# Norms by scaled tokens and plain transposes, attention heads placed ahead of the block-inverse merges

## The chip, the cores and the metric

The kernel runs on one core of one Trainium2 chip, as one launch. The metric is the device time of that core in microseconds (us). The kernel before was run three times: 1037.62, 1032.43 and 1036.91 us, median 1036.91. One more execution was recorded by the profiler; every row of a trace below is from that one.

## The reference, cut to what matters

All arithmetic is f32. The input is 256 tokens of width 1024. Three layers follow one another; the first two are layers 0 and 1 of a transformer (mixers of kind MLA and differential attention), the third is a hybrid of attention and a gated delta rule.

```python
def rms_norm(x, g):
    return x * rsqrt(mean(x * x, -1) + EPS) * g

for i in range(2):                                   # layers 0 and 1
    a = mixer_i(rms_norm(h, norm_g[i, 0]))           # MLA, then differential attention
    h = h + rms_norm(a, norm_g[i, 1])
    f = conv_ffn(rms_norm(h, norm_g[i, 2]))          # up 1024->5632, conv of width 3, gelu gate, down
    h = h + rms_norm(f, norm_g[i, 3])

# hybrid layer
p = rms_norm(h, pre_norm_w) @ w_in                   # q,k,v,z of two branches, beta, decay, two gates
o_a = causal_attention(rope(q_a), rope(k_a), v_a)    # 8 heads of 128
q_b, k_b, v_b = silu(causal_conv4(...))              # width 4, per channel
g = -exp(a_log) * softplus(decay + dt_bias);  beta = sigmoid(...)
# per head and chunk: strict lower triangular m[i,j] = beta_i k_i.k_j exp(G_i - G_j)
#   (I + m) is inverted, and the state passes from chunk to chunk
o_b = rms_norm(gated_delta_rule(q_b, k_b, v_b, g, beta), gdn_norm_w)
y = sigmoid(gate_a) * ((o_a * silu(z_a)) @ w_a) + sigmoid(gate_b) * ((o_b * silu(z_b)) @ w_b)
out = h + rms_norm(y @ w_out, post_norm_w)
```

## The kernel before

**Data.** The residual `h` has tokens on the partitions, in two blocks `tb` of 128 tokens. What a matmul consumes is transposed: `xT` has channels on the partitions, 8 tiles `kt` of 128 channels by 256 tokens. Nearly all products are done in three passes (`mm3`, lines 131 to 133): an f32 operand is split into a rounded high part `hi` and a remainder `lo`, and hi*hi, hi*lo and lo*hi are added. `wload` fetches weights from memory in 512 KB pieces through SyncE's queue into a ring of `RB = 5` slots; ScalarE makes the high part (L116), VectorE the low part (L117). `split` (L125) does the same for activations.

**A norm.** `boundary` stands between two stages. `postnorm` adds a stage's normed output to `h`. `prenorm` makes ready the next stage's normed input: ScalarE squares and sums (L199, in `square`), VectorE computes 1/rms in six small steps (`newton`, L208 to L221). Beside that, VectorE multiplies the left half of the tokens with the norm weight into `hg[0]` (L278) and GpSimd the right half into `hg[1]` (L279). VectorE then scales the identity by 1/rms into the diagonal `dg` (L282). `turn` multiplies each 128x128 piece of `hg` by `dg` on TensorE (L290): that scales and transposes in one product. The first norm has no weight of its own at this point; its `hg` is `h` itself, and the weight is put in behind the turn, as `gT`. There are five such norms (into MLA, FFN, differential attention, FFN, hybrid) of two token blocks each. The second block's `prenorm` stands behind the first block's splits (`ends`). In both FFN stages the first two column pairs of the up-projection run in plain f32 from `xF` (L602).

**The hybrid layer.** Eight times `h_kq` projections with their convolution; then for 2 chunks x 2 groups of 4 heads: decay matrices (L953 to L962), products k.k and k.q (L967), from them the matrices `A` and `Bm` (L971, L973), and `turn_A` (L946, L947), which transposes a group's `A` into `M` one group after it was made. `M`'s 16x16 diagonal blocks go through a scratch in memory (L985, L987), VectorE inverts them in 15 steps (L992, L993), the result goes through the scratch again, twice (L999, L1001), and is expanded to the block diagonal `V` and its transpose `VT` by a product with a mask (L1003; `V` on VectorE, `VT` on GpSimd). Then four projections `v_b`; three merge levels (L1038 to L1060) that grow the inverted blocks from 16 to 128; the delta rule's products (L1073); and eight attention heads (L1117 to L1157), each with a projection, rope (L1124 to L1127), softmax and products, and a gate projection `zproj` on every second one. After the heads come the two branches' projections and the output.

**Order.** The program is traced in the order of its text and a planner orders each engine's instructions by their place in the text and by its own model of when their inputs are ready; an instruction later in the text runs earlier when the one ahead isn't ready in that model. On the chip each engine and each DMA queue then runs its list in order. `behind(x)` forces the instructions in its block to stand after `x` on `x`'s engine.

Of the kernel before, what the change touches and what calls it, by code (L numbers as in the profile page):

```python
# [17 lines left out]
P = 128  # L18
# [19 lines left out]
def build(tc, a, out):  # L38
# [246 lines left out]
    def turn(tb, hg, dg, xT, xF=None):  # L285
# [466 lines left out]
    def hybrid(xT, fin):  # L752
        with ExitStack() as c2:
# [129 lines left out]
            last_mm = []  # L883
# [65 lines left out]
            pend = None  # L949
            for c in range(2):  # L950
                for gr in range(2):
# [46 lines left out]
            for src, sc, dst, eng in ((TBt, scr[2], V, nc.vector), (TB, scr[1], VT, nc.gpsimd)):  # L998
                nc.sync.dma_start(sc.rearrange("y b r s -> (y b) r s"), src)  # L999
                cb = lt("MB" if dst is V else "cbt", [P, 16, 16])  # L1000
                nc.sync.dma_start(cb, sc.rearrange("y b r s -> (b r) y s"))  # L1001
                for c in range(2):
                    eng.tensor_tensor(dst[:, c].rearrange("p n (b s) -> p n b s", b=8),  # L1003
                                      cb[:, 8 * c:8 * c + 8, None, :].to_broadcast([P, 8, 8, 16]),
                                      bmask.rearrange("p (b s) -> p b s", b=8)[:, None].to_broadcast([P, 8, 8, 16]),
                                      op=ALU.mult)

            def v_b(hp):
                b = proj2(wload(a["h_vb"][hp], 2048), (mmb, mmb, lambda: bank("s"), lambda: bank("s"))[hp])
                c = pair(0)  # L1010
                for t in range(2):
                    conv4(b[:, t], 16 + 2 * hp + t, c[:, t])
                th = pair(1)
                nc.scalar.activation(th, c, AF.Tanh, scale=0.5)
                nc.vector.scalar_tensor_tensor(c, th, 1.0, c, op0=ALU.add, op1=ALU.mult)
                for tb in range(2):
                    b = smb()
                    for t in range(2):
                        nc.tensor.transpose(b[:, t * P:(t + 1) * P], c[:, t, tsl[tb]], ident)
                    nc.vector.tensor_tensor(Vik[:, tb, 2 * hp:2 * hp + 2], b[:, :S].rearrange("p (t s) -> p t s", t=2),  # L1020
# [326 lines left out]
```

## Time and profile before

| | |
|---|---|
| median of 3 runs | 1036.91 us (1032.43 to 1037.62) |
| profiled execution | 1035.35 us, span 1033.4 us |
| TensorE matmul | busy 1008.6 us, 98% of the span, 7116 instructions |
| TensorE weight load | 923.6 us, 89% |
| VectorE | 739.4 us, 72% |
| ScalarE | 547.6 us, 53% |
| GpSimd | 33.3 us, 3% |
| memory traffic | 162.70 MB, 157 GB/s on average |
| granted TensorE clock | 0.995 of full on average |

Matmuls are pipelined: the busy time of one is its length from start to result, and the next begins before it ends. What a stream of them costs is read from the distance between starts. Waits and the chain of work that ended last say where another engine sets the pace.

### The profile page before, as it was taken

Reading aid. Unit: us, or ns where it says so; the run is one execution under the profiler, and the core shown is the slowest. Engines: PE = TensorE matmul, PEld = TensorE weight load, DVE = VectorE, ACT = ScalarE, POOL = GpSimd, SP = SyncE. Lnnn points to the kernel's source line nnn. Section 1 sums busy time; section 2 is a strip of 40 time slices with the busy share of each in tenths; the row PEclk is TensorE's granted clock in tenths of the full one; section 3 lists DMA queues with packets and bytes.
Section 4 is the critical chain, followed back from the end, with each engine's and each line's share of the span. In section 5 each row is a group of like instructions: output and inputs, shape, how many; then the busy total and the mean of one; then the engine's idle time right before and its main releaser. Section 6 shows DMA issues by size and latency. Waiting matters only on the chain.

```text
span 1033.4 us, 18142 instructions
## 1 busy us (share of the span) xinstructions
PE 1008.6 (98%) x7116; PEld 923.6 (89%) x7116; DVE 739.4 (72%) x1391; ACT 547.6 (53%) x955; POOL 33.3 (3%) x35
## 2 busy tenths in 40 slices
PE   9989899999999999999999999999999999999997
PEld 6878799999987887799999997899898999999996
DVE  6785688777667578778777767488799657675564
ACT  5653466555536456566555555565554455544451
POOL 0000100000011000010000001000203000000000
PEclk9999899999999999999999999999999999999999
DMA  8473477655435335367655442545244413455551
GB/s 280 148 238 110 145 226 213 188 185 165 135 96 200 136 102 183 96 235 229 209 189 187 146 143 75 172 156 174 71 146 101 132 61 115 151 184 184 185 164 42
DMA packets 55301, 162.70 MB, mean 157 GB/s; under 512 B 12784, under 2 KB 15280, under 8 KB 55216
## 3 DMA queue, kind: packets, MB, share of 16 engines
q1 hardware_dynamic: 55216, 161.55, 48.8%
q8 instruction: 56, 0.92, 0.4%
q14 instruction: 29, 0.24, 0.1%
HBM read 160.08 MB, written 1.44 MB: 156 GB/s over the span
## 4 chain that ended last, share of the span: by engine, by line
PE 85%; DVE 8%; ACT 3%; DMA 2%; issue 1%; SPq 0%; POOL 0%; DVEq 0%; ACTq 0%; POOLq 0%
PE mm L131 11%; PE mm L132 11%; PE mm L133 11%; PE acc L132 8%; PE acc L131 8%; PE acc L133 8%; PE sm L133 4%; PE sm L132 4%; PE sm L131 4%; PE mm L602 3%; PE acc L1038 2%; DVE lo L117 1%; PE acc L1073 1%; PE sm L290 1%; PE s L718 1%
## 5 line engine op out<-in xcount | busy, mean ns | idle before, releaser
L117 DVE TENSOR_TENSOR lo<-raw,hi 128x1024 fp32r<-128x1024 f32 (+1 forms) x271 | 326.8, 1209 | 137.6 <-ACT hi L116 136.4
L116 ACT CAST hi<-raw 128x1024 fp32r<-128x1024 f32 (+1 forms) x271 | 278.1, 1035 | 243.5 <-PE mm L132 126.4
L133 PE MATMUL mm<-xT,lo 128*128 128x256 f32 x928 | 265.7, 286 | 0.0
L131 PE MATMUL mm<-xT,hi 128*128 128x256 f32 x928 | 265.3, 286 | 0.0
L132 PE MATMUL mm<-xT,hi 128*128 128x256 f32 x928 | 265.0, 286 | 0.0
L132 PEld LDWEIGHTS mm<-xT,hi 128*128 128x128 f32 x928 | 177.6, 191 | 1.9 <-issue 0.7
L131 PEld LDWEIGHTS mm<-xT,hi 128*128 128x128 f32 x928 | 177.5, 191 | 1.5 <-issue 0.3
L133 PEld LDWEIGHTS mm<-xT,lo 128*128 128x128 f32 x928 | 177.6, 191 | 1.3 <-issue 0.7
L131 PE MATMUL sm<-xT,hi 128*128 128x256 f32 (+1 forms) x328 | 92.9, 283 | 0.0
L133 PE MATMUL sm<-xT,lo 128*128 128x256 f32 (+1 forms) x328 | 92.8, 283 | 0.0
L132 PE MATMUL sm<-xT,hi 128*128 128x256 f32 (+1 forms) x328 | 92.8, 283 | 0.0
L131 PE MATMUL acc<-hi,gv 128*128 128x512 f32 x176 | 69.2, 393 | 0.3 <-ACT gv L125 0.3
L132 PE MATMUL acc<-lo,gv 128*128 128x512 f32 x176 | 69.0, 392 | 0.0
L133 PE MATMUL acc<-hi,gv 128*128 128x512 f32 x176 | 68.5, 389 | 0.0
L132 PEld LDWEIGHTS sm<-xT,hi 128*128 128x128 f32 (+1 forms) x328 | 62.2, 190 | 0.9
L131 PEld LDWEIGHTS sm<-xT,hi 128*128 128x128 f32 (+1 forms) x328 | 62.2, 190 | 0.8
L133 PEld LDWEIGHTS sm<-xT,lo 128*128 128x128 f32 (+1 forms) x328 | 62.2, 190 | 0.1
L133 PEld LDWEIGHTS acc<-hi,gv 128*128 128x128 f32 x176 | 33.1, 188 | 7.5 <-DVE gv L125 0.3
L131 PEld LDWEIGHTS acc<-hi,gv 128*128 128x128 f32 x176 | 33.2, 189 | 6.6 <-ACT gv L125 1.0
L132 PEld LDWEIGHTS acc<-lo,gv 128*128 128x128 f32 x176 | 33.2, 189 | 5.3
L131 PE MATMUL mm<-og,hi 128*128 128x256 f32 x128 | 36.0, 281 | 0.0
L132 PE MATMUL mm<-og,hi 128*128 128x256 f32 x128 | 36.0, 281 | 0.0
(489 smaller groups left out, 1892.8 us busy)
## 6 DMA issues: line engine op xcount, KB each, us to landing
raw<-in_ffn_up SPq DMA_DIRECT2D x88, 512.0 KB, 4.7
raw<-in_ffn_down SPq DMA_DIRECT2D x44, 512.0 KB, 4.3
raw<-in_diff_qk SPq DMA_DIRECT2D x16, 512.0 KB, 5.0
raw<-in_h_kq SPq DMA_DIRECT2D x16, 512.0 KB, 4.6
raw<-in_h_qk SPq DMA_DIRECT2D x16, 512.0 KB, 4.3
raw<-in_h_z SPq DMA_DIRECT2D x16, 512.0 KB, 3.8
raw<-in_h_gate SPq DMA_DIRECT2D x16, 512.0 KB, 4.6
raw<-in_h_br SPq DMA_DIRECT2D x16, 512.0 KB, 4.6
```

The lines of the kernel that those rows point to most:

```text
L116: nc.scalar.copy(hi[:, :k], raw[:, :k])
L117: (eng or nc.vector).tensor_tensor(lo[:, :k], raw[:, :k], hi.bitcast(F32)[:, :k], op=ALU.subtract)
L131: nc.tensor.matmul(o, l[0], r[0], start=start, stop=False)
L132: nc.tensor.matmul(o, l[0], r[1], start=False, stop=False)
L133: return nc.tensor.matmul(o, l[1], r[0], start=False, stop=stop)
L290: nc.tensor.matmul(b[:, i * P:(i + 1) * P], hg[f][:, i * P:(i + 1) * P], dg, start=True, stop=True)
L602: last = nc.tensor.matmul(mmf[j][:, t, tsl[tb]], raws[j][t][:, kt * P:kt * P + P], xF[kt // 4][:, kt % 4, tsl[tb]], start=kt == 0, stop=kt ...
L718: nc.tensor.matmul(sb, q[:, tsl[tb]], kb, start=True, stop=False)
L1038: nc.tensor.matmul(b[:, i], lhs(i), rhs(i), start=True, stop=True)
L1073: nc.tensor.matmul(b[:, i], lhs(hds[i], i), rhs(hds[i], i), start=True, stop=True)
```

## The change

In `prenorm`, 1/rms is computed first; then VectorE puts 1/rms and norm weight onto both halves of the tokens in one instruction each. In the first norm, which has no weight there, VectorE scales the left half and ScalarE the right one. The diagonal is gone, GpSimd has no part in norms any more, and `turn` transposes with the identity. In the hybrid layer, `turn_A` runs two groups behind, the last two behind the two halves of the first `v_b` projection, which now stands ahead of the scratch transfers; both expansions are VectorE's, chunk by chunk; and the loop over the attention heads is cut: heads 0 to 2 stand ahead of the merges (whose first products stand behind the projection of head 2), heads 3 to 7 where all eight stood. The code of `v_b`, of the merges, of the delta rule's products and of a head is moved and otherwise unchanged.

```diff
     def prenorm(tb, g_bc, aft, warm_):
-        hg = [xp.tile([P, 512], F32, tag=f"hg{tb}{f}", name=nm("hg"), bufs=1) if g_bc is not None else h[:, tb, hf[f]] for f in range(2)]
+        hg = [xp.tile([P, 512], F32, tag=f"hg{tb}{f}", name=nm("hg"), bufs=1) for f in range(2)]
...
+        with behind(*aft):
+            r = newton(ss, 2, D)
         if g_bc is not None:
-            with behind(*aft):
-                last = nc.vector.tensor_tensor(hg[0], h[:, tb, hf[0]], g_bc[:, hf[0]], op=ALU.mult)
-            nc.gpsimd.tensor_tensor(hg[1], h[:, tb, hf[1]], g_bc[:, hf[1]], op=ALU.mult)
-        r = newton(ss, 2, D)
-        dg = xp.tile([P, P], F32, tag="dg", name=nm("dg"), bufs=2)
-        last = nc.vector.tensor_scalar(dg, ident, r, None, op0=ALU.mult)
-        return (hg, dg), [last]
+            for f in range(2):
+                last = nc.vector.scalar_tensor_tensor(hg[f], h[:, tb, hf[f]], r, g_bc[:, hf[f]], op0=ALU.mult, op1=ALU.mult)
+        else:
+            last = nc.vector.tensor_scalar(hg[0], h[:, tb, hf[0]], r, None, op0=ALU.mult)
+            nc.scalar.activation(hg[1], h[:, tb, hf[1]], AF.Identity, scale=r)
+        return (hg,), [last]
     def turn(tb, hg, xT, xF=None):
...
-                nc.tensor.matmul(b[:, i * P:(i + 1) * P], hg[f][:, i * P:(i + 1) * P], dg, start=True, stop=True)
+                nc.tensor.transpose(b[:, i * P:(i + 1) * P], hg[f][:, i * P:(i + 1) * P], ident)
...
     def proj2(w, bk=mmb):
...
+                    half_mm[t:] = last_mm
...
-                    if pend is not None:
+                    if len(pend) == 2:
                         with behind(lq):
-                            turn_A(*pend)
-                    pend = (c, gr)
-            turn_A(*pend)
+                            turn_A(*pend.pop(0))
+                    pend.append((c, gr))
+            v_b(0)
+            for p_, m_ in zip(pend, half_mm):
+                with behind(m_):
+                    turn_A(*p_)
...
-            for src, sc, dst, eng in ((TBt, scr[2], V, nc.vector), (TB, scr[1], VT, nc.gpsimd)):
+            cbs = []
+            for src, sc, dst in ((TBt, scr[2], V), (TB, scr[1], VT)):
                 nc.sync.dma_start(sc.rearrange("y b r s -> (y b) r s"), src)
-                cb = lt("MB" if dst is V else "cbt", [P, 16, 16])
-                nc.sync.dma_start(cb, sc.rearrange("y b r s -> (b r) y s"))
-                for c in range(2):
-                    eng.tensor_tensor(dst[:, c].rearrange("p n (b s) -> p n b s", b=8), ...
+                cbs.append(lt("MB" if dst is V else "cbt", [P, 16, 16]))
+                nc.sync.dma_start(cbs[-1], sc.rearrange("y b r s -> (b r) y s"))
+            for c in range(2):
+                for cb, dst in zip(cbs, (V, VT)):
+                    nc.vector.tensor_tensor(dst[:, c].rearrange("p n (b s) -> p n b s", b=8), ...
-            for hp in range(4):
+            for hp in range(1, 4):
                 v_b(hp)
...
-            for hd in range(H):
+            def moba(hd):
                 b = proj2(wload(a["h_qk"][hd], 2048))
+                ends_qk.append(last_mm[0])
...
+            for hd in range(3):
+                moba(hd)
             for lev in range(3):
...
+                        with behind(*(ends_qk[2:] if lev + c + gr == 0 else ())):
+                            b = mm4h(lambda i: M[:, c, 4 * gr + i, r], lambda i: half(V[:, c, 4 * gr + i], 1))
...
+            for hd in range(3, H):
+                moba(hd)
```

## Rows read from the trace of the kernel before

**Rows 1.** The page's parts 1 and 4: busy time, share, instructions; the chain.
```profile
PE 1008.6 (98%) x7116; PEld 923.6 (89%) x7116; DVE 739.4 (72%) x1391; ACT 547.6 (53%) x955; POOL 33.3 (3%) x35
...
PE 85%; DVE 8%; ACT 3%; DMA 2%; issue 1%; SPq 0%; POOL 0%; DVEq 0%; ACTq 0%; POOLq 0%
```

**Rows 2.** Who TensorE waited for: us in total, times, longest.
```profile
PE sm L290 <- DVE dg L282: 1.8, 2, 1.5
PE acc L1038 <- DVE A L1003: 1.8, 1, 1.8
...
PE acc L132 <- DVE lo L117: 1.4, 1, 1.4
PE acc L132 <- DVE A L117: 1.2, 1, 1.2
PE acc L946 <- DVE Bm L973: 0.8, 1, 0.8
```

**Rows 3.** Timeline (start us, us, what): one whole turn; four transposes in a merge.
```profile
308.97 1.95 PE L290 MATMUL mm<-dg,hg 128*128 128x128 f32 x16
...
804.21 0.60 PE L1057 MATMUL acc<-c_ident,A 128*128 128x128 f32 x4
```

**Rows 4.** VectorE's groups by form: busy us, mean ns, idle before.
```profile
L117 DVE TENSOR_TENSOR lo<-raw,hi 128x1024 fp32r<-128x1024 f32 x261 | 319.3, 1226 | 137.4 <-ACT hi L116 136.2
...
L241 DVE SCALAR_TENSOR_TENSOR h<-yg,s,h 128x512 f32<-128x512 f32 x18 | 13.5, 750 | 0.8
...
L278 DVE TENSOR_TENSOR hg<-h,gain 128x512 f32<-128x512 f32 x8 | 5.9, 738 | 0.0
...
L238 DVE TENSOR_TENSOR yg<-acc,gain 128x512 f32<-128x512 f32 x8 | 5.5, 690 | 11.1 <-ACT junk L199 11.1
...
L282 DVE TENSOR_SCALAR dg<-c_ident,s 128x128 f32<-128x128 f32 x10 | 2.9, 290 | 0.3
```

**Rows 5.** The first step of 1/rms, L208: ns min/median/max, first and last start.
```profile
L208 DVE SCALAR_TENSOR_TENSOR s<-s x20: 146/160/924, 4.8 to 1027.3; 128x1 f32<-128x1 f32 x20
```

**Rows 6.** Stretch from MLA to FFN: engines' busy us, granted clock, DMA.
```profile
111.28:118.11 6.83, 5.36 (x25) 5.16 (x25) 5.92 (x19) 3.10 (x7) 0.71 (x2) 0.50 0.97 361
```

**Rows 7.** Timeline from MLA to FFN, first token block.
```profile
112.61 0.29 DVE L282 TENSOR_SCALAR dg<-c_ident,s 128x128 f32<-128x128 f32 x1
...
112.95 3.78 PE L290 MATMUL sm<-dg,hg 128*128 128x128 f32 x16 [1.47 <-DVE dg L282]
116.52 0.85 PE L602 MATMUL mm<-xF,raw 128*128 128x128 f32 x3
```

**Rows 8.** Timeline from differential attention to FFN, both token blocks.
```profile
444.45 5.66 PE L602 MATMUL mm<-xF,raw 128*128 128x128 f32 x48
450.14 2.02 PE L290 MATMUL sm<-dg,hg 128*128 128x128 f32 x16
```

**Rows 9.** Timeline of VectorE from FFN to differential attention.
```profile
314.91 2.31 DVE L117 TENSOR_TENSOR lo<-raw,hi 128x1024 fp32r<-128x1024 f32 x1
...
322.45 0.28 DVE L282 TENSOR_SCALAR dg<-c_ident,s 128x128 f32<-128x128 f32 x1
```

**Rows 10.** Timeline of VectorE and GpSimd around the expansion.
```profile
784.96 0.66 DVE L1126 TENSOR_TENSOR pr<-pr,rC 32x512 f32<-32x512 f32 x1
...
786.28 7.79 POOL L1003 TENSOR_TENSOR VT<-cbt,h_bmask 128x1024 f32<-128x1024 f32 x2 [39.21 <-DMA cbt<-scr]
...
786.69 2.86 DVE L1127 TENSOR_TENSOR pr<-pr,sw 32x512 f32<-32x512 f32 x1
789.48 2.34 DVE L1003 TENSOR_TENSOR A<-MB,h_bmask 128x1024 f32<-128x1024 f32 x2
```

**Rows 11.** Timeline of ScalarE and SyncE's queue: last M, weight loads, third head.
```profile
749.75 0.59 ACT L947 COPY M<-acc 128x512 f32<-128x512 f32 x1 [1.74 <-PE acc L946]
...
765.44 13.80 SPq L110 DMA_DIRECT2D raw<-in_h_qk  x3
...
787.14 0.58 ACT L1121 COPY pr<-mm 128x512 f32<-128x512 f32 x1
```

More of the change, by code (lines that the diff above doesn't have):

```diff
@@ L947, in turn_A @@
                 nc.scalar.copy(M[:, c, 4 * gr:4 * gr + 4], b)
-            pend = None
+            pend = []
             for c in range(2):
@@ L1008, in v_b @@
-            def v_b(hp):
-                b = proj2(wload(a["h_vb"][hp], 2048), (mmb, mmb, lambda: bank("s"), lambda: bank("s"))[hp])
-                c = pair(0)
-                for t in range(2):
[L1012 to L1015, printed above, removed]
-                for tb in range(2):
[L1017 to L1020, printed above, removed]
-                                            hik[:, tb, 2 * hp:2 * hp + 2, None].to_broadcast([P, 2, P]), op=ALU.mult)
@@ L1023, in hybrid @@
[L1023 to L1024 removed]
+                cbs.append(lt("MB" if dst is V else "cbt", [P, 16, 16]))
+                nc.sync.dma_start(cbs[-1], sc.rearrange("y b r s -> (b r) y s"))
+            for c in range(2):
+                for cb, dst in zip(cbs, (V, VT)):
+                    nc.vector.tensor_tensor(dst[:, c].rearrange("p n (b s) -> p n b s", b=8),
+                                            cb[:, 8 * c:8 * c + 8, None, :].to_broadcast([P, 8, 8, 16]),
+                                            bmask.rearrange("p (b s) -> p b s", b=8)[:, None].to_broadcast([P, 8, 8, 16]),
+                                            op=ALU.mult)
@@ new lines, in hybrid, with zproj @@
+            for hp in range(1, 4):
+                v_b(hp)
+            def zproj(br, hp):
+                b = proj2(wload(a["h_z"][br, hp], 2048))
+                th = pair(1)
+                nc.scalar.activation(th, b, AF.Tanh, scale=0.5)
+                nc.vector.scalar_tensor_tensor(th, th, 1.0, b, op0=ALU.add, op1=ALU.mult)
+                return th
+            scale = P ** -0.5
+            swap = [(p + 16) % 32 for p in range(32)]
+            zs, ends_qk = [], []
+            def moba(hd):
+                b = proj2(wload(a["h_qk"][hd], 2048))
+                ends_qk.append(last_mm[0])
+                qk = pair(0)
+                nc.scalar.copy(qk, b)
+                sw = lt("sw", [32, 2, S])
+                for t in range(2):
+                    nc.vector.stream_shuffle(sw[:, t], qk[:32, t], swap)
+                nc.vector.tensor_tensor(sw, sw, rS[:, None, :].to_broadcast([32, 2, S]), op=ALU.mult)
+                nc.vector.tensor_tensor(qk[:32], qk[:32], rC[:, None, :].to_broadcast([32, 2, S]), op=ALU.mult)
+                nc.vector.tensor_tensor(qk[:32], qk[:32], sw, op=ALU.add)
+                sb = bank("s")
+                nc.tensor.matmul(sb[:, 0:P], qk[:, 0, tsl[0]], qk[:, 1, 0:P], start=True, stop=False)
+                nc.tensor.matmul(sb[:, 0:P], idb, mA, start=False, stop=True)
+                nc.tensor.matmul(sb[:, P:3 * P], qk[:, 0, tsl[1]], qk[:, 1], start=True, stop=False)
+                nc.tensor.matmul(sb[:, 2 * P:3 * P], idb, mA, start=False, stop=True)
+                mx = small(2, F32, "mx")
+                sm = small(2, F32, "smx")
+                e = lt("ea", [P, 3, P], bufs=2)
+                ev = e.rearrange("p a b -> p (a b)")
+                rg = [slice(0, P), slice(P, 3 * P)]
+                for tb in range(2):
+                    nc.vector.tensor_reduce(mx[:, tb:tb + 1], sb[:, rg[tb]], axis=AX.X, op=ALU.max)
+                nc.vector.tensor_scalar(mx, mx, -scale, None, op0=ALU.mult)
+                for tb in range(2):
+                    nc.scalar.activation(ev[:, rg[tb]], sb[:, rg[tb]], AF.Exp, bias=mx[:, tb:tb + 1], scale=scale,
+                                         accum_out=sm[:, tb:tb + 1])
+                rs = small(2, F32, "rsx")
+                nc.vector.tensor_scalar(sm, sm, 2.0, None, op0=ALU.mult)
+                nc.vector.reciprocal(rs, sm)
+                for tb in range(2):
+                    nc.scalar.activation(ev[:, rg[tb]], ev[:, rg[tb]], AF.Identity, scale=rs[:, tb:tb + 1])
+                pT = lt("pTa", [P, 3, P], bufs=2)
+                tposes([e[:, i] for i in range(3)], pT, eng="s")
+                pv = pT.rearrange("p a b -> p (a b)")
+                ob = bank("s")
+                nc.tensor.matmul(ob[:, :S], va[:, 0, hd * P:(hd + 1) * P], pv[:, 0:S], start=True, stop=False)
+                nc.tensor.matmul(ob[:, P:S], va[:, 1, hd * P:(hd + 1) * P], pv[:, S:3 * P], start=False, stop=True)
+                if hd % 2 == 0:
+                    zs[:] = [zproj(0, hd // 2)]
+                nc.vector.tensor_tensor(oza[:, hd], ob[:, :S], zs[0][:, hd % 2], op=ALU.mult)
@@ L1044, in hybrid @@
                         Pm = w5()
-                        b = mm4h(lambda i: M[:, c, 4 * gr + i, r], lambda i: half(V[:, c, 4 * gr + i], 1))
+                        with behind(*(ends_qk[2:] if lev + c + gr == 0 else ())):
+                            b = mm4h(lambda i: M[:, c, 4 * gr + i, r], lambda i: half(V[:, c, 4 * gr + i], 1))
                         d = halves(Pm, 1)
```

70 lines of the change are left out of this document (16 added, 54 removed).

## The prediction

> **What bounds the kernel now.** I read the shares of the engines first, then the chain that ended last, then what TensorE waited for, and only then the stages that the change touches. TensorE is busy in 98% of the span and carries 85% of the chain [rows 1]; no other engine comes near. TensorE idles for 24.8 us in all (1033.4 less 1008.6), and the waits that this change can reach are five: 1.8 us before the norm's matmuls, 1.4 and 1.2 us for a weight's low half just after a norm, 1.8 us for the expanded inverse, 0.8 us for a transpose in front of the scratch transfers [rows 2]. So an edit is worth what it takes off TensorE's stream, plus the few waits that it removes, less what VectorE then delivers later. The sum is made against the profiled execution: 1035.35 us, its span 1033.4 and 1.95 around it. The median of the runs shown, 1036.91, lies 1.56 us above.
>
> **TensorE's part of the norms.** A turn brings one token block's 128x1024 values to channels by eight products with the diagonal of 1/rms, and each is an f32 product that runs as two instructions: 16 of them take 1.95 us, of which the last one's own length is 0.275, so one follows the other after (1.95 - 0.275) / 15 = 0.112 us [rows 3]. A transpose is one instruction: four take 0.60, so (0.60 - 0.277) / 3 = 0.108 each [rows 3]. A turn thus falls from 16 x 0.112 = 1.79 to 8 x 0.108 = 0.86, and ten turns (five norms, two token blocks) give 9.3 us at most. Not all of it reaches the end.
>
> **VectorE's part of the norms.** Gone are one 128x512 product with the norm weight (0.74, made before 1/rms was known) and the diagonal (0.29); new are two products of the form of L241, 0.75 each, both after 1/rms [rows 4]. The path from 1/rms to the second half's operand grows from 0.29 to 1.50, to the first half's from 0.29 to 0.75. Against that GpSimd's product goes away. While it runs, the first step of the 1/rms chain is held: 0.92 at worst against a median of 0.16 [rows 5], in the four first blocks of the later norms. That returns 0.75 us of path.
>
> **Norm by norm.**
> - *Start* (no weight; VectorE scales one half, ScalarE the other). A 128x512 scaling lies between the 128x128 one's 0.29 and L241's 0.75 [rows 4], I take 0.5, in place of the diagonal's 0.29; ScalarE has weight casts around its half. The first block I take at nothing (between -0.9 and +0.6), the second, in the middle of a running stream, at nearly the full 0.93: **-0.8**.
> - *MLA to FFN.* Here TensorE really waits, and its clock falls: 0.50 granted for 6.83 us [rows 6], after TensorE had mostly stood still. The 16 products take 3.78 and the first up-projection begins beside the last of them, at 116.52 [rows 7]. After the change 1/rms is there 0.75 earlier, at 111.9; the halves at 112.6 and 113.4; transposes at half clock between 0.108 and twice that each, so the second half is turned by 114.3 and the projections run from about 114.6. That is 2 us earlier, but at half clock, worth 1.0. The second block's turn gives 0.9: VectorE, from 113.4, has two products by the weight (0.69 each), two chains to 1/rms (1.25 each: six small steps of 0.16 and their gaps), two additions (0.75) and two splits (0.69) to do, 6.7 us, and then the first half: 120.9. TensorE comes after 48 projections of 0.112, of which 3.5 us at half clock: 118.1 + 5.4 - 1.75 = 121.7. **-1.9** (between 0 and -3).
> - *FFN to diff.* TensorE is covered by the late down-projections, so the first turn only shortens the step to the cast, and then TensorE stands behind VectorE's weight halves. One of those took 2.31 instead of 1.23 beside GpSimd's product [rows 4, 9]; without it that wait [rows 2] shrinks. But the diagonal came at 322.45 at the end of an unbroken VectorE queue; five weight halves, the 1/rms chain and 1.5 us of products in its place end at about 323.2, so the second turn gets its operands as late as now and is merely shorter. **-1.4** (0 to -2.8).
> - *Diff to FFN.* The first turn: L208 loses 0.75, the path gains 0.46, and the first half's matmuls shorten by half, (0.90 to 0.44), so projections start at 443.7 instead of 444.45 [rows 8], -0.75. The second block is the place where the cover is gone: VectorE's same 6.7 us begin at 442.9, with the second half of the first block, and end at 449.6; the halves follow at 450.4 and 451.1. The transposes start about 450.4, not 450.14, while TensorE is free from 443.7 + 5.4 = 449.1. What is queued behind the turn on TensorE, 16 projections of the first block, may be put ahead. **-0.8** (+0.4 to -1.9).
> - *FFN to hybrid.* As FFN to diff; VectorE has 1.79 us of norm work there before and 1.50 after (0.74 + 0.29 + 0.76 of stretch, against 2 x 0.75), so the 1.2 us wait [rows 2] stays about half. **-1.0** (+0.5 to -2.5).
>
> Sum of the norms: -5.9 of 9.3.
>
> **The hybrid layer.** No instruction of TensorE is added or removed. (a) The transposes of A stand one group later, the last two behind the halves of the first v projection: the 0.8 us wait and a 0.2 beside it go; the price is that the last M, copied at 749.75 [rows 11], comes about 3 us later, and with it eight scratch writes, the read-back and the 15 steps of the block inverse. (b) Expansion: VT's two products move to VectorE, where such a one takes 1.21, so +2.4; but GpSimd's ran 7.79 us and held a small VectorE product for 2.86 where its neighbours take 0.66 [rows 10], -2.2. Nothing, net, on VectorE, and VT comes earlier than from GpSimd. (c) Three attention heads stand in front of the merges. In the trace TensorE already works on heads 0 to 2 (the third one's queries and keys are copied at 787.14 [rows 11]) when the merges begin, so this mainly fixes an order that the planner had found, and lets TensorE be busy when V arrives. The 1.8 us wait goes, if V is in time. The chain M to V is 3 later and 2.2 faster, so V lands about where it does now. I take **-2.5** out of the 2.8 us of waits, bounds +2 and -5 (other small stalls in this layer).
>
> **Sum.** -5.9 - 2.5 = -8.4: 1035.35 becomes 1026.95, a ratio of 0.9919, and against the median of the runs 1028.5.
>
> **A rule that speaks against it.** The trace shows the clock at 0.50 for 6.83 us after a stretch with nothing but short bursts on TensorE, and at full again after projections had run without a break [rows 6, 7]; no row shows what a run of transposes does to it. The Trainium skill, "TensorE: Matmul & The Clock Gate", Part 4: PE-mode transpose, says that the full clock doesn't engage for transposes, since they do not count as busy the way products do. By that, the turns at places with little else on TensorE would lower the clock or hold it low; that is the first rival below.
>
> **Rivals.**
> 1. *The clock falls where it did not.* At the start and at diff to FFN the turn is nearly all that TensorE does for 2 us; if the clock falls there for as long as at MLA to FFN, each costs 6.83 x 0.5 = 3.4 us [rows 6]: -8.4 + 6.8 = -1.6, or 1035.3. For it: only the products are replaced. Against: transposes stand for 1 us only, with projections right behind.
> 2. *VectorE takes the place of the products.* If at every second block the operands come later by the 1.2 us by which their path grows, the second turns give nothing (4 x 0.9) and the early gains wait behind them: norms -2, total -4.5, or 1032.4. For it: VectorE's unbroken queue at 314 to 324. Against: at two of four places TensorE has other work in hand.
> 3. *V comes late: slower.* The scratch transfers stand in SP's queue with weight loads that wait for a free slot; the trace has three loads spread over 13.8 us there [rows 11]. If the later M puts the read-back behind such a load, the merges' first product, and all TensorE work queued behind it, wait. It decides from V landing 8.4 us after TensorE wants it; at 12 us the total is +3.6 to +4, or 1041. Against: the planner orders SP's queue and knows the slots.
> 4. *The reorder does nothing.* Heads 0 to 2 were ahead already; then the norms alone, 1031.0; this lies in the main case's own range.
>
> **How the numbers follow.** Main case 0.60, own range 1023 to 1032; rival 1 0.10; rival 2 0.17; rival 3 0.08; 0.05 for more, where the clock stays up at MLA to FFN too (-8.4 - 3.4, or 1025 and below with luck elsewhere). A measurement of this kernel can tell 0.5%, 5.2 us, from no change: faster is below 1031.7. Main case nearly all, rival 2 by half: 0.70 faster, 0.21 same, 0.09 slower. The range 1021 to 1037 leaves out rival 3 and some of the best.
>
> **What would show it.** L290 with one instruction per tile, about 0.87 us a turn, and the operand "dg" gone: step 1. L208 nowhere above 0.3 us: the stretch by GpSimd is gone. The clock row: 0.50 only between MLA and FFN; any other stretch is rival 1. At each second block, TensorE's wait before L290 for "hg": over 1 us at three places is rival 2. L1038's first wait: gone, or several us (rival 3). It is wrong if TensorE's instructions shrink by 80 and the span by less than 4 us.

## The result and the profile after

Before, 6 runs beside the changed kernel's have a median of 1034.95 us; the changed kernel's 6 have 1027.4 (1025.88 to 1028.97). The ratio is 0.9928, with a 95% interval from 0.9913 to 0.9944: 7.5 us less. The profiled execution of the changed kernel took 1028.22 us, its span 1026.4, at a granted clock of 0.997 on average.

The page's busy times and its chain, against [rows 1]:

```profile
PE 1000.8 (98%) x7034; PEld 913.4 (89%) x7036; DVE 737.5 (72%) x1393; ACT 549.8 (54%) x957; POOL 13.8 (1%) x25
...
PE 83%; DVE 9%; ACT 3%; DMA 2%; issue 2%; SPq 0%; POOLq 0%; DVEq 0%; ACTq 0%
```

TensorE shows 82 instructions fewer (80 by the text; a trace can lack a few) and is busy 7.8 us less, about what the span lost (7.0). GpSimd lost 19.5 us of work, and VectorE's busy time did not grow. What TensorE waited for (us in total, times, longest), against [rows 2]:

```profile
PE sm L292 <- DVE hg L280: 1.7, 2, 1.2
...
PE mm L292 <- DVE hg L280: 1.1, 1, 1.1
...
PE acc L132 <- DVE M L117: 0.8, 1, 0.8
PE acc L956 <- DVE Bm L976: 0.8, 1, 0.8
PE acc L132 <- DVE A L117: 0.8, 1, 0.8
PE acc L949 <- DVE A L974: 0.7, 1, 0.7
```

In place of the waits for the diagonal (1.8 in all) stand waits for the scaled halves `hg` (1.7 and 1.1); the 1.8 us for the expanded inverse (L1038, now L1102) is gone. Of the waits for a weight's low half just after a norm, the 1.4 (FFN to diff) is gone and the 1.2 (FFN to hybrid) has become two of 0.8 (`A` and `M`). In the hybrid layer the 0.8 us for `Bm` now stands in front of a decay matrix's first product (L956), not of a transpose, and the wait for `A` in front of the last transposes (L949) is 0.7 where it was 0.2. Lines moved a little: L290 is now L292, L602 is L604, L1003 is L1026.

VectorE's two norm products (group by form), and the first step of 1/rms (ns min/median/max, first and last start), against [rows 4, 5]:

```profile
L280 DVE SCALAR_TENSOR_TENSOR hg<-h,s,gain 128x512 f32<-128x512 f32 x16 | 11.4, 753 | 0.3
```

```profile
L208 DVE SCALAR_TENSOR_TENSOR s<-s x20: 150/159/161, 4.8 to 1020.1; 128x1 f32<-128x1 f32 x20
```

The products cost the 0.75 that the form of L241 cost, and L208, 0.92 at worst before, is never above 0.161: with GpSimd's product the hold is gone. By their groups, VectorE's norm products and its two added expansion products are about 6 us more work than before; that its busy time still fell by 1.9 means that its other instructions took some 8 us less together.

From MLA to FFN (timeline; then a stretch with each engine's busy time, the granted clock, DMA), against [rows 6, 7]:

```profile
109.03 0.16 DVE L208 SCALAR_TENSOR_TENSOR s<-s 128x1 f32<-128x1 f32 x1 [0.85 <-ACT junk L199]
...
110.31 1.42 DVE L280 SCALAR_TENSOR_TENSOR hg<-h,s,gain 128x512 f32<-128x512 f32 x2
...
111.12 1.78 PE L292 MATMUL sm<-c_ident,hg 128*128 128x128 f32 x8 [1.24 <-DVE hg L280]
112.69 8.19 PE L604 MATMUL mm<-xF,raw 128*128 128x128 f32 x62
...
120.72 0.60 PE L292 MATMUL sm<-c_ident,hg 128*128 128x128 f32 x4
```

```profile
111.28:115.00 3.72, 3.72 (x19) 3.47 (x19) 3.39 (x11) 2.14 (x4) 0.00 (x0) 0.54 1.01 403
```

The first turn is 1.78 long where it was 3.78, and the granted clock is at 0.50, the lower of its two levels (1.2 of 2.4 GHz), for 3.41 us here (111.59 to 115.00; the stretch shown begins 0.3 earlier), not for 6.83.

From FFN to diff and from diff to FFN (timelines of VectorE and TensorE), against [rows 8, 9]:

```profile
314.66 1.22 DVE L117 TENSOR_TENSOR lo<-raw,hi 128x1024 fp32r<-128x1024 f32 x1
...
317.88 1.41 DVE L280 SCALAR_TENSOR_TENSOR hg<-h,s,gain 128x512 f32<-128x512 f32 x2
...
318.78 0.41 PE L292 MATMUL mm<-c_ident,hg 128*128 128x128 f32 x2 [1.08 <-DVE hg L280]
...
438.85 5.57 PE L604 MATMUL mm<-xF,raw 128*128 128x128 f32 x48
444.91 1.29 PE L292 MATMUL sm<-c_ident,hg 128*128 128x128 f32 x8 [0.49 <-DVE hg L280]
```

The weight half that took 2.31 beside GpSimd's product takes 1.22; at both second blocks TensorE stands for `hg`, 1.08 and 0.49 us (the first row shows two of the turn's eight transposes), and then turns in 1.29 us at the latter place, where it took 2.02 [rows 8].

Around the expansion (timelines of VectorE, ScalarE and TensorE), against [rows 10, 11]:

```profile
743.15 0.59 ACT L950 COPY M<-acc 128x512 f32<-128x512 f32 x1 [1.50 <-PE acc L949]
...
780.15 1.21 DVE L1026 TENSOR_TENSOR VT<-cbt,h_bmask 128x1024 f32<-128x1024 f32 x1
781.29 2.34 DVE L1026 TENSOR_TENSOR A<-MB,h_bmask 128x1024 f32<-128x1024 f32 x2
783.56 1.21 DVE L1026 TENSOR_TENSOR VT<-cbt,h_bmask 128x1024 f32<-128x1024 f32 x1
...
785.03 0.67 DVE L1056 TENSOR_TENSOR pr<-pr,sw 32x512 f32<-32x512 f32 x1
...
786.88 1.06 PE L1102 MATMUL acc<-A,M 128*128 128x64 f32 x8
```

All four expansion products follow one another on VectorE and end at 784.8; the merges begin 2 us later and do not wait. The small rope product that took 2.86 beside GpSimd takes 0.67.

**Where the time came from, stage by stage.** Every trace has the same 5706 three-pass products (L131 to L133), so the start of the n-th can be compared between two traces. The differences to the kernel before, by stage, in us (changed kernel and four experiments, told below; each from one execution):

| | forecast | changed | norms alone | hybrid alone | products, not transposes | heads behind merges |
|---|---|---|---|---|---|---|
| start | -0.8 | -0.7 | -0.8 | -0.6 | -0.3 | -1.1 |
| in MLA | 0 | -0.9 | -0.2 | -0.3 | -0.4 | -0.3 |
| MLA to FFN | -1.9 | -2.5 | -3.4 | -1.7 | -2.3 | -3.4 |
| clock low there, us (6.83 before) | 6.83 | 3.41 | none | none | none | none |
| FFN to diff | -1.4 | -1.4 | -1.6 | 0 | -0.4 | -1.3 |
| in diff | 0 | +0.4 | -0.2 | 0 | 0 | +0.6 |
| diff to FFN | -0.8 | -0.8 | -0.8 | 0 | -0.1 | -0.8 |
| FFN to hybrid | -1.0 | -0.8 | -1.0 | 0 | -0.1 | -1.0 |
| hybrid | -2.5 | -0.4 | +1.6 | 0 | +1.2 | -1.9 |
| sum | -8.4 | -7.2 | -6.3 | -2.7 | -2.4 | -9.2 |

How far a single execution can be read: seven traces (the changed kernel twice, experiments 1, 5, 6, 7 and 9) are of kernels whose text is the same up to the hybrid layer. They span -0.5 to -1.3 at the start, -0.1 to -0.9 in MLA and -0.4 to +0.6 in diff, but only -1.3 to -1.5 at FFN to diff, -0.8 to -0.9 at diff to FFN and -0.8 to -1.0 at FFN to hybrid. These last three are firm. The start is not: with the norms as before (hybrid alone) it reads -0.6 too, so no run shows that the norm made the -0.7 there.

### The profile page after: what moved, and what is told of

Its sections match the earlier page's. It is cut to its first block, busy times and chain, and to the rows that moved or that the text cites. A ratio compares the mean times of both kernels' runs of the same rounds, so it can differ in the third digit from the quotient of the medians.

```text
span 1026.4 us, 17963 instructions
## 1 busy us (share of the span) xinstructions
PE 1000.8 (98%) x7034; PEld 913.4 (89%) x7036; DVE 737.5 (72%) x1393; ACT 549.8 (54%) x957; POOL 13.8 (1%) x25
## 4 chain that ended last, share of the span: by engine, by line
PE 83%; DVE 9%; ACT 3%; DMA 2%; issue 2%; SPq 0%; POOLq 0%; DVEq 0%; ACTq 0%
PE mm L131 11%; PE mm L132 11%; PE mm L133 11%; PE acc L131 8%; PE acc L132 8%; PE acc L133 7%; PE sm L133 4%; PE sm L132 4%; PE sm L131 4%; PE mm L604 2%; PE acc L1102 2%; DVE lo L117 2%; PE acc L1138 1%; PE s L720 1%; PE sm L173 1%
## 5 line engine op out<-in xcount | busy, mean ns | idle before, releaser
L117 DVE TENSOR_TENSOR lo<-raw,hi 128x1024 fp32r<-128x1024 f32 (+1 forms) x271 | 325.6, 1205 | 133.1 <-ACT hi L116 132.0
L133 PE MATMUL mm<-xT,lo 128*128 128x256 f32 x928 | 265.9, 287 | 0.0
L131 PE MATMUL mm<-xT,hi 128*128 128x256 f32 x928 | 264.7, 285 | 0.0
L131 PEld LDWEIGHTS mm<-xT,hi 128*128 128x128 f32 x928 | 177.5, 191 | 1.5 <-issue 0.3
L133 PEld LDWEIGHTS mm<-xT,lo 128*128 128x128 f32 x928 | 177.5, 191 | 1.2 <-issue 0.7
L131 PE MATMUL sm<-xT,hi 128*128 128x256 f32 (+1 forms) x328 | 92.8, 283 | 0.0
L133 PE MATMUL sm<-xT,lo 128*128 128x256 f32 (+1 forms) x328 | 92.8, 283 | 0.0
L131 PE MATMUL acc<-hi,gv 128*128 128x512 f32 x176 | 69.2, 393 | 0.0
L133 PE MATMUL acc<-hi,gv 128*128 128x512 f32 x176 | 68.5, 389 | 0.0
L131 PEld LDWEIGHTS sm<-xT,hi 128*128 128x128 f32 (+1 forms) x328 | 62.2, 190 | 0.8
L133 PEld LDWEIGHTS sm<-xT,lo 128*128 128x128 f32 (+1 forms) x328 | 62.2, 190 | 0.1
L133 PEld LDWEIGHTS acc<-hi,gv 128*128 128x128 f32 x176 | 33.0, 188 | 7.5 <-DVE gv L125 0.3
L131 PEld LDWEIGHTS acc<-hi,gv 128*128 128x128 f32 x176 | 33.2, 189 | 6.3 <-ACT gv L125 0.6
L131 PE MATMUL mm<-og,hi 128*128 128x256 f32 x128 | 36.0, 281 | 0.0
```

The source lines that it names most:

```text
L117: (eng or nc.vector).tensor_tensor(lo[:, :k], raw[:, :k], hi.bitcast(F32)[:, :k], op=ALU.subtract)
L131: nc.tensor.matmul(o, l[0], r[0], start=start, stop=False)
L133: return nc.tensor.matmul(o, l[1], r[0], start=False, stop=stop)
```

## The experiments

Ratios are to the kernel before, with 95% intervals. The first four ran on one chip, then four on another, then four on a third.

**1. The norms alone**: the changed `prenorm` and `turn`, and the hybrid layer as before.

> The norms' part of the change alone; the hybrid layer as before. Theory 1 (read from the two traces: TensorE is 6.8 us ahead when the hybrid layer begins and 7.2 us at the end): nearly all of the gain is the norms', so 6 to 7 us less than before, ratio 0.9935. Rival (the prediction's split, -5.9 and -2.5): 5 to 6 us less, and the hybrid part alone gives 2 to 3. Rival 2 (the clock's low stretch between MLA and FFN was merely shorter in the one profile): 3 to 5 us less, with the low stretch as long as before.

Measured: 1028.89 us, ratio 0.9936 (0.9917 to 0.9956), 6.6 us less by the ratio and 5.6 by the medians. The norms carry most of the gain; the interval (4.6 to 8.6) can't tell 6 to 7 from 5 to 6. In this trace the clock stayed up between MLA and FFN, and fell elsewhere, where TensorE stood for the expanded inverse (timeline of TensorE; the stretch behind it):

```profile
782.89 1.33 PE L1040 MATMUL acc<-A,M 128*128 128x64 f32 x8 [1.80 <-DVE A L1005]
```

```profile
783.59:787.00 3.41, 3.41 (x18) 3.41 (x18) 1.83 (x7) 1.05 (x1) 2.61 (x1) 0.51 0.04 12
```

3.41 us at half the clock can cost up to 1.7, and the hybrid stage in this kernel's column is +1.6. The fall came 0.7 us after the wait; that the wait set it off is likely, not shown.

**2. The hybrid part alone**: norms as before.

> The hybrid layer's part alone; the norms as before. Theory 1: the 1.8 us wait for the expanded inverse goes, but the waits in front of the decay matrices stay under another name, so 0 to 1 us less, ratio 0.9995 and not to be told from 1. Rival (the prediction): 2 to 3 us less, ratio 0.9975.

Measured: 1033.38 us, 0.9985 (0.9973 to 0.9998). Small, and in its trace the hybrid stage is not shorter at all; the 2.7 us that this execution gains lie at the start, in MLA, and in the clock, which happened to stay up between MLA and FFN. The clock has a hand in the timing too: the 12 runs had a granted clock of 0.998 on average (median of the runs), before's 23 beside them 0.995, and among runs at 0.998 or more the medians are 1033.04 (9 runs) and 1033.89 (5). Whether the reorder itself keeps the clock up isn't shown. With the first experiment the two parts add up within the intervals (-6.6 and -1.6 against -7.5).

**3. Products in place of the transposes**, all else as changed.

```diff
-                nc.tensor.transpose(b[:, i * P:(i + 1) * P], hg[f][:, i * P:(i + 1) * P], ident)
+                nc.tensor.matmul(b[:, i * P:(i + 1) * P], hg[f][:, i * P:(i + 1) * P], ident, start=True, stop=True)
```

> The changed kernel, with each transpose of a turn made as an f32 product with the identity: 80 instructions of TensorE come back, VectorE's and ScalarE's part stays as in the changed kernel. Theory 1 (TensorE's stream is the price): 5 to 9 us of the gain are lost, 1033 to 1035. Rival (the gain came from the shorter way to 1/rms without GpSimd): 1 to 3 us are lost, 1028.5 to 1030.5.

Measured: 1033.42 us, 0.9975 (0.9961 to 0.9989); by the ratios 4.9 us above the changed kernel. A turn in a busy stretch, between FFN and diff, first of this kernel, then of the changed one (timelines):

```profile
305.94 1.95 PE L292 MATMUL mm<-c_ident,hg 128*128 128x128 f32 x16
```

```profile
304.87 1.03 PE L292 MATMUL mm<-c_ident,hg 128*128 128x128 f32 x8
```

0.92 per turn, 0.93 worked out from [rows 3]. By stages, against the norms alone: 0.5 at the start, 1.1, 1.2, 0.7, 0.9 at the four others, 4.4 of the norms' gain. Two turns take 1.84 us off TensorE in each stage, so from a quarter to two thirds of that arrives. What VectorE's new order brings without the cheaper turn is about 1.4 (0.3, 0.5 besides the clock, 0.4, 0.1, 0.1). The two figures of the start are within its spread. Besides, the hybrid stage is 1.6 longer than in the changed kernel, by one wait behind a merge (timeline):

```profile
797.06 0.84 PE L173 MATMUL sm<-c_ident,ea 128*128 128x128 f32 x3 [1.72 <-ACT ea L1077]
```

These are a softmax's transposes of a head that the change put ahead of the merges: TensorE has come to them before ScalarE has made the weights `ea`. In the changed kernel that wait is 0.2. No other trace has it so long (0.7 at most), and why ScalarE was late here is not traced.

**4. The right half's weight put on before 1/rms is known**, 1/rms by ScalarE behind it.

```diff
...
-            for f in range(2):
-                last = nc.vector.scalar_tensor_tensor(hg[f], h[:, tb, hf[f]], r, g_bc[:, hf[f]], op0=ALU.mult, op1=ALU.mult)
+            with behind(*aft):
+                nc.vector.tensor_tensor(hg[1], h[:, tb, hf[1]], g_bc[:, hf[1]], op=ALU.mult)
+                r = newton(ss, 2, D)
+            last = nc.vector.scalar_tensor_tensor(hg[0], h[:, tb, hf[0]], r, g_bc[:, hf[0]], op0=ALU.mult, op1=ALU.mult)
+            nc.scalar.activation(hg[1], hg[1], AF.Identity, scale=r)
...
```

> The changed kernel, with the right half's norm weight put on by VectorE before 1/rms is known and 1/rms put on it by ScalarE, while VectorE does the left half: the second operand comes some 0.65 us after 1/rms instead of 1.5. Theory 1 (TensorE's remaining waits for these operands, 2.8 us in the changed kernel, are VectorE's two products in a row): 1 to 2 us less than the changed kernel, about 1026. Rival: the product before 1/rms delays 1/rms by as much, and ScalarE is busy then: no difference within 0.5 us, or up to 1 us more.

Measured: 1027.31 us, 0.992 (0.990 to 0.9941): no different from the changed kernel. The second half's path is shorter, but TensorE's waits for the left half are no shorter (L295 waits 1.8 us in two and 1.5 in one for `hg`): that half now comes later, since the product ahead of 1/rms delays 1/rms (timelines of VectorE and TensorE at the second block, FFN to diff; in the changed kernel's trace, which is 0.4 us further ahead by then, 317.88 and 318.78):

```profile
318.66 0.75 DVE L280 SCALAR_TENSOR_TENSOR hg<-h,s,gain 128x512 f32<-128x512 f32 x1
...
319.56 1.06 PE L295 MATMUL mm<-c_ident,hg 128*128 128x128 f32 x8 [1.50 <-DVE hg L280]
```

By stages in its trace it is 0.4 worse than the changed kernel at FFN to diff and at diff to FFN, and 0.8 better at FFN to hybrid.

**5. VT's expansion back on GpSimd.**

```diff
-                for cb, dst in zip(cbs, (V, VT)):
-                    nc.vector.tensor_tensor(dst[:, c]...
+                for cb, dst, eng in zip(cbs, (V, VT), (nc.vector, nc.gpsimd)):
+                    eng.tensor_tensor(dst[:, c]...
```

> The changed kernel, with VT's two expansion products back on GpSimd and V's two left on VectorE. Theory (the two engines hold each other, so the move to VectorE costs VectorE nothing and brings VT earlier): GpSimd's two products take about 3.9 us each again, V's second product on VectorE 2.3 instead of 1.2, a small VectorE product beside them over 2 us; VT comes about 3 us later than in the changed kernel, and the merges' second products wait up to 2 us for it; time +0.5 to +2 us against the changed kernel, 1028 to 1029.5. Rival (TensorE has heads 0 to 2 in hand, so it is indifferent who expands): the holds come back in the rows, but the time is the changed kernel's within 0.3 us.

Measured: 1029.45 us, 0.9945 (0.9927 to 0.9963); 1.2 to 1.8 us above the changed kernel by the ratios (that has 0.9933 in a second series, experiment 12), with intervals that overlap. In the trace the hybrid stage is 1.1 longer than before, not 0.4 shorter. Two of VectorE's rows are held again (2.87 where it was 0.67, 2.35 where it was 1.21: 3.3 us together, against the 2.4 that VT's two products take on VectorE), and TensorE waits 1.7 us for VectorE's `oza` (timelines of GpSimd and VectorE; TensorE's wait). V's two products are not held, which I had expected of the second: they take 2.34 together, as in the changed kernel.

```profile
778.60 7.78 POOL L1026 TENSOR_TENSOR VT<-cbt,h_bmask 128x1024 f32<-128x1024 f32 x2 [39.33 <-DMA cbt<-scr]
...
779.02 2.87 DVE L1056 TENSOR_TENSOR pr<-pr,sw 32x512 f32<-32x512 f32 x1
781.82 2.34 DVE L1026 TENSOR_TENSOR A<-MB,h_bmask 128x1024 f32<-128x1024 f32 x2
...
785.12 2.35 DVE L117 TENSOR_TENSOR lo<-raw,hi 128x1024 fp32r<-128x1024 f32 x1
```

```profile
PE s L1058 <- DVE oza L1086: 1.7, 1, 1.7
```

**6. The heads written behind the merges**: expansion and transposes of A as changed.

```diff
-            for hd in range(3):
-                moba(hd)
...
-                        with behind(*(ends_qk[2:] if lev + c + gr == 0 else ())):
+                        if True:
...
-            for hd in range(3, H):
+            for hd in range(H):
```

> The changed kernel, with all eight attention heads written behind the merges as before the change, and the expansion and the transposes of A left as changed. Theory (it is the heads ahead of the merges that took away TensorE's 1.8 us wait for V): that wait is back, 1 to 2 us, and the time is 1 to 2 us above the changed kernel. Rival 1 (the planner puts the heads there by itself, and V's earlier arrival removed the wait): no wait for V, time within 0.5 us of the changed kernel. Rival 2 (the fixed order costs more than it brings): 1 us below the changed kernel.

Measured: 1026.65 us, 0.9922 (0.9904 to 0.994). No wait for V: with VectorE's expansion the heads ahead are not needed for that (nor, with the heads ahead, is VectorE's expansion: experiment 5 has no such wait either). In the trace the hybrid stage is 1.9 shorter than before, 1.5 better than with the heads ahead. In the changed kernel TensorE pauses three times around the third head's softmax among the merges, between 791.9 and 793.6, by 0.17, 0.29 and 0.26 over the usual distance of starts (timeline of the changed kernel: three transposes that take 0.84; 0.109 apart they would take 0.5):

```profile
792.18 0.84 PE L173 MATMUL sm<-c_ident,ea 128*128 128x128 f32 x3
```

Those are gone, 0.7 of the 1.5. The rest is spread over many steps, and I have no single cause for it. The difference itself repeats: the seven traces with three heads ahead of the merges and no other edit in the hybrid layer (the changed kernel twice, experiments 2, 3, 4, 8 and 10) read -0.5 to +1.2 there, the two with the heads behind (6 and 11) -1.9 and -2.0.

**7. The strict mask by VectorE instead of GpSimd.**

```diff
-                    nc.gpsimd.tensor_tensor(Ds, Dm, strict...
+                    nc.vector.tensor_tensor(Ds, Dm, strict...
```

> The changed kernel, with the four 128x512 products by the strict mask moved from GpSimd to VectorE. Theory (beside GpSimd's mask products two VectorE steps in front of the decay matrices take 0.72 and 1.25 instead of 0.19, and the last A waits 1.2 us for a mask product): on VectorE the four cost 0.74 each, about 3.0 us, 1.6 come back from the held steps, and TensorE's two stalls in front of the transposes (0.95 and 0.85) shrink to under 0.4 each: 0.5 to 1.5 us below the changed kernel. Rival (VectorE is without a break busy in this stretch and its queue is what TensorE waits for): VectorE's 1.4 us more stand in front of A, the stalls grow by as much, and the time is 0 to 1.5 us above the changed kernel.

Measured: 1032.09 us, 0.9977 (0.9966 to 0.9989): some 5 us worse than the changed kernel, far more than either theory had. The two stalls that I aimed at are gone from TensorE's waits, but V is made at 783.8, not 781.3: the inverse's last step begins 0.9 later on VectorE, and its way through the scratch ends later still, so that VectorE stands 1.58 us for it. TensorE then waits 2.1 us inside the merges, and the clock falls (timelines of VectorE and TensorE; the stretch):

```profile
783.77 2.36 DVE L1026 TENSOR_TENSOR A<-MB,h_bmask 128x1024 f32<-128x1024 f32 x2 [1.58 <-DMA MB<-scr]
...
788.72 1.97 PE L1102 MATMUL acc<-w,VT 128*128 128x64 f32 x8 [2.06 <-DVE w L1113]
```

```profile
788.49:795.31 6.82, 5.54 (x21) 4.74 (x22) 4.56 (x10) 3.25 (x9) 0.00 (x0) 0.50 0.09 15
```

The fall is not this one execution's: the granted clock of its 12 runs is 0.994 (median of the runs' averages; none at 0.998), that of the changed kernel's six 0.9975.

**8. 160 transposes in a row**, added behind the products at the start; their result is not used.

```diff
+        b_ = smb()
+        for i in range(160):
+            nc.tensor.transpose(b_[:, i % 4 * P:i % 4 * P + P], ident, ident)
```

> The changed kernel, with 160 transposes of the identity in a row added on TensorE, right behind the products that stand at the start and ahead of the first turn; their result isn't used. If transposes keep the clock as products do: the granted clock goes up where it does now, at 5.8 us, and stays at 1.00 through the run; the transposes follow one another after 0.109 us, the run takes 17.4 us. If the rule holds that transposes don't count as busy: within the run the granted clock falls to 0.50 and the pitch becomes about twice as long until products follow; the run takes 25 us or more. The time of the kernel is longer by the run, less what the first weights' arrival hides.

Measured (timeline; stretch): one run, 1042.64 us.

```profile
6.46 17.63 PE L1239 MATMUL sm<-c_ident 128*128 128x128 f32 x160
```

```profile
6.33:24.00 17.67, 17.67 (x163) 17.59 (x162) 6.94 (x8) 6.63 (x8) 0.00 (x0) 1.00 0.99 335
```

(17.63 - 0.273) / 159 = 0.109 us from first to last, at a granted clock of 1.00 throughout. Transposes alone kept a clock that was already up for 17 us; whether they would raise it from 0.50 was not tried. The rule of the Trainium skill that spoke against the change ("TensorE: Matmul & The Clock Gate", Part 4: PE-mode transpose: transposes do not count as busy) is not borne out by this trace, as far as holding the clock goes.

**9. The transposes of A where they were.**

```diff
-                    if len(pend) == 2:
+                    if len(pend) == 1:
...
+            turn_A(*pend.pop(0))
             v_b(0)
-            for p_, m_ in zip(pend, half_mm):
-                with behind(m_):
-                    turn_A(*p_)
```

> The changed kernel, with the transposes of A back where they were: each group's right behind the next group's products, the last one's ahead of the first v projection. Theory (the later place only exchanges one short wait for another, and M's last copy comes no later by it): TensorE waits some 0.9 us for Bm and 0.4 for A before these transposes, as before the change, instead of 0.95 and 0.85 now; V lands within 1 us of where it does in the changed kernel, no wait for V; time within 0.7 us of the changed kernel. Rival (the transposes of A carry what the hybrid part gained): 1 to 2 us above the changed kernel.

Measured: 1026.38 us, 0.9927 (0.9914 to 0.994), beside 1026.84 for the changed kernel on that chip. The hybrid stage is 0.5 shorter than before, against 0.4. No effect of this step shows either way.

**10. Pauses filled** with transposes of the identity between MLA and FFN.

```diff
...
+                fill(b_, more[f])
...
+                    more = (14, 5, 12) if post and post[1] == 1 else (0, 0, 0)
+                    if more[0]:
+                        with behind(mids[0]):
+                            fill(smb(), more[0])
...
```

> The changed kernel, with TensorE kept going while it waits between MLA and FFN: 14, 5 and 12 transposes of the identity, results unused, in the three pauses ahead of the first turn (1.6, 0.6 and 1.2 us), each 0.109 us. Theory (the clock's fall there is set off by these pauses, and comes and goes from run to run): no stretch at 0.50 between MLA and FFN in any run, the turn's eight transposes and the projections behind it run at full clock, the granted clock is 0.998 or 0.999; the time is 0.5 to 2 us below the changed kernel's median, at its fastest runs (1025.9), and the runs lie closer together. Rival 1 (the fall depends on something else): stretches at 0.50 stay, no gain. Rival 2 (the added work holds up the turn): TensorE reaches the turn later than its operands, 0.5 to 1.5 us slower.

Measured: 1026.81 us, 0.9937 (0.9923 to 0.995), beside 1026.84. In its trace the clock stays up, the turn and the projections behind it run at full clock, and then TensorE stands for the second block (timeline):

```profile
110.81 1.32 PE L300 MATMUL sm<-c_ident,hg 128*128 128x128 f32 x8
112.14 6.07 PE L616 MATMUL mm<-xF,raw 128*128 128x128 f32 x52
118.84 0.41 PE L300 MATMUL sm<-c_ident,hg 128*128 128x128 f32 x2 [0.63 <-DVE hg L288]
```

The stage from MLA to FFN reads -3.0 here, between the -2.5 of the changed kernel's two traces (clock low for 3.41 us) and the -3.4 of experiments 1, 5, 6, 8 and 9, where the clock stayed up by itself. In the time no gain shows. The runs lie hardly closer together (their spans 1024.7 to 1026.1, those of the changed kernel on that chip 1024.4 to 1026.3); that this fall makes the spread of the runs is not borne out by these few.

**11 and 12. Filled pauses and heads behind the merges together; the changed kernel once more.**

> The kernel with the filled pauses and, besides, the heads written behind the merges. If the two are independent and the heads' place is worth what it seemed to be (0.75 us in favour of behind the merges, not resolved), this is 0.5 to 1 us below the one with filled pauses alone, 1025 or less; if that difference was chance, it is equal to it.

> The changed kernel itself, beside the other three on the same chip, so that differences below 1 us can be read: 1027.4 plus or minus 0.7; its profile has a stretch at 0.50 between MLA and FFN of none, 3.4 or 6.8 us.

Measured: 1025.36 us, 0.9918 (0.9903 to 0.9933), and 1026.84, 0.9933 (0.9919 to 0.9946). As the filled pauses alone bring nothing that the time shows, the 1.5 us are put down to the heads' place, as in the trace of experiment 6. The intervals overlap; that the version with the heads behind the merges beats the changed kernel is likely (by 0.6 to 1.1 us in the ratios of experiment 6, by 1.5 here, and by 1.5 in the hybrid stage of both traces), and by the times alone not settled.

## Why the prediction held, and where it did not

The forecast was 1028.5 and a ratio of 0.9919; measured are 1027.4 and 0.9928. The sum of -8.4 stands against -7.5. (That 1027.4 lies below 1028.5 although less was gained comes from before's median, 1036.91 in three runs and 1034.95 in six.) The nearness of the sum is in part luck: the trace's -7.2 holds 0.8 to 0.9 from the clock's shorter low stretch and 0.9 in MLA that nothing in the change accounts for, and they stand in for 2 us that the hybrid layer did not give.

**TensorE's part of the norms: right.** 0.93 per turn forecast, 1.95 - 1.03 = 0.92 measured.

**Norm by norm: right in size at four places, not shown at the start.** In the three places that the clock does not touch: -1.4, -0.8, -1.0 forecast, -1.4, -0.8, -0.8 in the changed kernel and -1.6, -0.8, -1.0 with the norms alone. One step behind these is wrong: at FFN to hybrid I had the 1.2 us wait for a weight half shrink to about half, and it became two waits, 0.76 and 0.79, since VectorE's two norm products now stand between the two weight halves (L117 of `A` at 638.12, L280 at 639.26, L117 of `M` at 640.59). At MLA to FFN the first projection begins at 112.69; with the 1.6 us that the trace was ahead by then, that is 114.3 in before's time, where the forecast had 114.6, and the second turn, at 122.3, stands against 121.7. The stage's -2.5 instead of -1.9 is the clock's shorter low stretch, which I had taken as fixed; in experiment 7's trace, with the same text up to there and 6.83 us low as before, the stage reads -1.8. It is not fixed: of the ten traces with changed norms and unfilled pauses it was low there for 6.83 us in two, for 3.41 in two, and not at all in six. With the clock up in both kernels (experiments 1 and 2) the norm alone is worth 3.37 - 1.75 = 1.6 there, and without the clock the norms give 0.8 + 1.6 + 1.6 + 0.8 + 1.0 = 5.8, against 5.9 forecast; the 0.8 of the start in it is not shown to be the norm's, which leaves 5.0 to 5.8.

**The hybrid layer: mis-sized.** -2.5 forecast; -0.4 in the trace, -1.6 by the timing of that part alone, with an interval from -0.2 to -2.8, some of which goes with the clock (experiment 2). All three of its steps went otherwise than I wrote. By the traces they come to about 0, -1.9 and +1.5:
- *(a) the transposes of A.* M's last copy did not come 3 us later: 743.15, and 6.8 ahead at that point, is 749.95 in before's time, where it was 749.75. The 0.8 wait in front of a transpose did go, but waits of 0.8 for Bm at the next decay matrix and 0.7 for A took its place. Experiment 9: no effect.
- *(b) the expansion.* I set +2.4 against -2.2 and called it even. It is the step that carries this part: with the heads behind the merges, where it is what is left besides (a), the hybrid stage is 1.9 and 2.0 shorter (experiments 6 and 11). V is then in time even so, since its first product starts at 781.29, or 788.1 in before's time, against 789.48 [rows 10]; before, the held rope product (2.86) stood right in front of it in VectorE's queue. Taking VT's half back costs 1.2 to 1.8 us by the ratios (experiment 5), a size that the intervals don't settle; there the hold fell on two rows, not on the one that I had priced.
- *(c) the heads ahead.* I took it for an order that the planner had anyway. It is not free: heads behind the merges are 1.5 better in the trace. About half of that is seen: softmax transposes that no longer stand in TensorE's list ahead of their weights (0.7); the cause of the rest stays open.

**The rivals.** The first, the clock: the granted clock is 1.00 from 5.77, where its record begins, to 111.59, and again through diff to FFN, and experiment 8 takes its ground away for a clock that is up. Its price, and that of the clock staying up at MLA to FFN, was too high: I had 3.4 us for 6.83 us at 0.50, and the traces give 1.7 (experiment 2 against before) and 1.6 (experiment 7 against 1). The second, VectorE late at the second blocks: TensorE's waits for `hg` above 1 us are two, only one of them (1.08, FFN to diff, ending at 318.78) in front of a second block; so it happened at one place of four. The third, V late: no. But the direction had something: in experiment 7 V was 2.5 later, and the wait and the clock together made the hybrid stage 3.6 us longer than in the changed kernel. I had set the point from which it decides at 8.4 us of lateness, and had left the clock out of its price. The fourth, that the reorder does nothing, is nearly what the trace shows (-0.4); by the timing of that part alone it gives something (-0.2 to -2.8).

The marks that I named came as named: one instruction per tile, 82 instructions of TensorE and 7.0 us of the span gone, L208 nowhere above 0.3, the first wait of L1038 gone, 0.50 in the middle of the kernel only between MLA and FFN.

## What to carry to other kernels

Where TensorE is busy 98% of the time, what counts is what an operation takes off its stream: a transpose instead of an f32 product with a diagonal halves a step. But it paid in full nowhere: of 1.84 us per pair of turns 0.5 to 1.2 arrived (experiment 3 against 1). Where the rest went is not traced beyond TensorE's waits for the scaled operands, 2.8 us in the changed kernel and 2.0 in experiment 3. Before moving work to a second engine, look at what the neighbour's rows beside it take: GpSimd's products cost VectorE more than they saved it (VectorE has about 6 us of work more, and its busy time fell by 1.9). And a fixed order is a change with a price of its own; try it apart from what it came with.

## What the runs showed that I had not expected

- The clock's low stretch between MLA and FFN is 0, 3.41 or 6.83 us long in executions of the same text up to there, and its price is half of what half a clock would take: 1.7 us for 6.83 before the change (experiment 2 against before), 0.8 to 0.9 for 3.41 after it (the changed kernel's two traces against experiment 1). A longer wait of TensorE for the second block is only a part of that: 0.32 us in experiment 2, none before. The rest is not traced.
- A wait of about 2 us in the merges was followed by 3.4 or 6.8 us at half clock (experiments 1 and 7); before's own trace had the same 1.8 us wait [rows 2] without a fall.
- A 32x512 product on VectorE took 2.87 us beside GpSimd's 128x1024 one and 0.67 without it.
